# The first feed-forward's gate and up weights: every fourth float32r remainder summed by an accumulating DMA from SBUF

## The chip, the cores and the metric

The kernel runs on one core of one Trainium2 chip. The metric is the device time of one execution in microseconds (us), lower is better. The core's engines run side by side, each with its own instruction stream: TensorE (PE: matmuls; PEld: its weight loads), VectorE (DVE), ScalarE (ACT), GpSimd (POOL) and SyncE (SP, which here only issues loads). They wait for each other through semaphores. Sixteen DMA engines move the data for all of them.

## The reference, cut to what matters

One layer of a Conformer-like block over 256 tokens of width 2048: a first feed-forward, a mixing sublayer, cross-attention and a second feed-forward. The change touches the first half of the first feed-forward:

```python
h = rms_norm(x, ffn1_norm[l])
gate, up = jnp.split(h @ w_in, 2, axis=-1)          # w_in: 2048 x 11264
x = x + 0.5 * ((jax.nn.silu(gate) * up) @ w_out)    # w_out: 5632 x 2048
```

## The kernel before

All weights are float32 in HBM. TensorE multiplies float32r, a shorter float format, so every operand is split in two: `hi` is the value rounded to float32r, `lo` is the remainder `x - hi`, again rounded. Each product is then three matmuls: `hi` by `hi`, `hi` by `lo`, `lo` by `hi`.

The function `weights` makes such a pair for one weight tile of 128 x 1024 (512 KB): SP issues the load into a tile `raw` (four buffers), ACT copies it rounded into the first half of a tile `hl` (L104, three buffers), DVE subtracts that from `raw` into the second half (L105).

Gate and up of a feed-forward are computed by `swiglu_in` in 11 groups (`j`) of 512 gate and 512 up columns. A group takes 16 K tiles (`k`), each one load of 128 x 1024. For each K tile `by_two` issues 12 matmuls of 512 columns into four PSUM accumulators: four of line L258 (`hi` of the weights), four of L259 (`lo` of the weights), four of L262 (`lo` of the activations by `hi` of the weights). At the end of a group ACT applies SiLU to the gate (L274), DVE multiplies by up (L275), and PE transposes the result (L288) during the next group. The first group of the first feed-forward is written apart, in `first_group`: there the input `x` is loaded and split as well. Both feed-forwards call `swiglu_in`; `first` is not None in the first alone.

The order on each engine is set by the framework's scheduler when the kernel is built. Every instruction keeps its place in its engine's stream, so one that waits holds back all behind it.

Of the kernel before, what the change touches and what calls it, by code (L numbers as in the profile page):

```python
# [11 lines left out]
F32 = mybir.dt.float32  # L12
F32R = mybir.dt.float32r
AF = mybir.ActivationFunctionType
ALU = mybir.AluOpType
AX = mybir.AxisListType

P = 128
# [4 lines left out]
KD = D // P  # L23
# [38 lines left out]
def layer(ctx: ExitStack, tc: tile.TileContext, a: dict):  # L62
    nc = tc.nc
    out = a["out"]
# [19 lines left out]
    def beside(us):  # L84
        budget[0] = min(budget[0] + us, us) if later else 0.0
        while later and budget[0] > 0:
            cost, part = later.popleft()
            with tc.issue_after(newest[0].ins):
                part()
            budget[0] -= cost  # L90
# [6 lines left out]
    def weights(src, kk, n, hl=None):  # L97

        raw = wraw.tile([P, 1024], F32, name="raw")
        size = kk * n  # L100
        nc.sync.dma_start(out=raw[:, :size].rearrange("p (k n) -> p k n", n=n), in_=src)
        if hl is None:
            hl = whl.tile([P, 2, 1024], F32R, name="hl")
        nc.scalar.copy(out=hl[:, 0, :size], in_=raw[:, :size])  # L104
        newest[0] = nc.vector.tensor_tensor(  # L105
            out=hl[:, 1, :size], in0=raw[:, :size], in1=hl[:, 0, :size].bitcast(F32), op=ALU.subtract
        )
        v = hl[:, :, :size].rearrange("p two (k n) -> p two k n", n=n)
        return v[:, 0], v[:, 1]

    def split(hi, lo, x):
        nc.scalar.copy(out=hi, in_=x)
        nc.vector.tensor_tensor(out=lo, in0=x, in1=hi.bitcast(F32), op=ALU.subtract)
# [13 lines left out]
    def product_part(acc, w, k0, kk, x_hl, per, first, last, joint=False):  # L127

        hi, lo = weights(w[:, k0:k0 + kk, :], kk, P)
        for k in range(kk):  # L130
            f, l = first and k == 0, last and k == kk - 1
            (product_joint if joint else product)(acc, hi[:, k], lo[:, k], x_hl(k0 + k), f, l)
        beside(per)

    def gemm_t(w, x_hl, per=0.0, acc=None, ks=None, joint=False, between=None):

        return ahead([w], x_hl, per, [acc], ks, joint, between=between)[0]
# [14 lines left out]
    def gemm_n(w, x_hl, per=0.0, between=None):  # L152

        acc = [ps.tile([P, 2, 256], F32, name="acc").rearrange("p a b -> p (a b)") for _ in range(2)]
        nk = w.shape[1]
        for k0 in range(0, nk, 2):
            kk = min(2, nk - k0)
            hi, lo = weights(w[:, k0:k0 + kk, :], kk, 512)
            for k in range(kk):
                x = x_hl(k0 + k)  # L160
                for t in range(2):
                    s = slice(t * P, (t + 1) * P)
                    nc.tensor.matmul(acc[t], lhsT=x[:, 0, s], rhs=hi[:, k], start=k0 + k == 0, stop=False)  # L163
                    nc.tensor.matmul(acc[t], lhsT=x[:, 0, s], rhs=lo[:, k], start=False, stop=False)  # L164
                    nc.tensor.matmul(acc[t], lhsT=x[:, 1, s], rhs=hi[:, k], start=False, stop=k0 + k == nk - 1)  # L165
            if between and k0 >= 4:
                between.pop(0)()
            beside(per)
        return acc
# [65 lines left out]
    def gained_tile(norm):  # L235

        return big.tile([P, KD, 2, T], F32R, name="x_hl", tag="S")
# [11 lines left out]
    G = 512  # L249
    NG = F // G  # L250

    def by_two(acc, x, hi, lo, first, last):

        for t in range(2):
            s = slice(t * P, (t + 1) * P)
            for g in range(2):
                c = slice(g * G, (g + 1) * G)
                nc.tensor.matmul(acc[t][g], lhsT=x[:, 0, s], rhs=hi[:, c], start=first, stop=False)  # L258
                nc.tensor.matmul(acc[t][g], lhsT=x[:, 0, s], rhs=lo[:, c], start=False, stop=False)  # L259
            for g in range(2):  # L260
                c = slice(g * G, (g + 1) * G)
                nc.tensor.matmul(acc[t][g], lhsT=x[:, 1, s], rhs=hi[:, c], start=False, stop=last)  # L262

    def token_accs():
        return [[ps.tile([P, 2, 256], F32, name="acc").rearrange("p a b -> p (a b)") for _ in range(2)] for _ in range(2)]

    def swiglu_in(pool, x_hl, root, w_in, hA, hB, first, per):

        turns = []

        def gated(acc, r):
            h = pool.tile([P, 2, G], F32, name="h", bufs=2)
            for t in range(2):
                nc.scalar.activation(out=h[:, t], in_=acc[t][0], func=AF.Silu, scale=r[:, t:t + 1])  # L274
                nc.vector.scalar_tensor_tensor(  # L275
                    out=h[:, t], in0=acc[t][1], scalar=r[:, t:t + 1], in1=h[:, t], op0=ALU.mult, op1=ALU.mult
                )
            return h

        def turn(j, h, half):  # L280
            def go():
                f = 4 * j + 2 * half
                dst = hA[:, f:f + 2] if f < KD else hB[:, f - KD:f - KD + 2]
                tp = pa.tile([P, 2, T], F32, name="aux")
                for k in range(2):
                    for t in range(2):
                        c = slice((2 * half + k) * P, (2 * half + k + 1) * P)
                        nc.tensor.transpose(out=tp[:, k, t * P:(t + 1) * P], in_=h[:, t, c], identity=ident)  # L288
                split(dst[:, :, 0], dst[:, :, 1], tp)
            return go  # L290

        r = None
        for j in range(NG):
            if j == 0 and first is not None:
                acc = first()
            else:
                acc = token_accs()
                for k in range(KD):
                    hi, lo = weights(w_in[j, :, k:k + 1], 1, 2 * G)
                    by_two(acc, x_hl[:, k], hi[:, 0], lo[:, 0], k == 0, k == KD - 1)  # L300
                    if k in (3, 5) and turns:
                        turns.pop(0)()
                    beside(per)
            if r is None:
                r = root()
            h = gated(acc, r)
            turns += [turn(j, h, half) for half in range(2)]
        return turns

    def h_of(hA, hB):  # L310
        return lambda k: hA[:, k] if k < KD else hB[:, k - KD]


    x_hl = gained_tile("ffn1_norm")
# [31 lines left out]
    with tc.tile_pool(name="ffn1", bufs=1) as pool:  # L346
# [20 lines left out]
        x_hl = gained_tile("mix_norm")  # L367
        ss = st.tile([P, T], F32, name="ss", bufs=2)
        for f in range(KD):
            if f == 0:  # L370
                acc = gemm_t(a["ffn1_w_out"][f], h_of(hA, hB), between=turns)
            else:
                acc = gemm_t(a["ffn1_w_out"][f], h_of(hA, hB))
# [3 lines left out]
    with tc.tile_pool(name="mid", bufs=1) as mid:  # L377
        kT = mid.tile([P, KD, M], F32, name="kT")
        vv = mid.tile([P, 2, D], F32, name="vv")
        with tc.tile_pool(name="mix", bufs=1) as pool:  # L380
# [122 lines left out]
            for n in range(2):  # L503
                acc = gemm_n(a["w_mix_v"][n], lambda k: x_hl[:, k], per=1.35)
                for t in range(2):
                    nc.scalar.activation(
                        out=vs[:, t, n * 512:(n + 1) * 512], in_=acc[t], func=AF.Gelu, scale=r_t[:, t:t + 1]
# [57 lines left out]
            for f in range(KD):  # L565
                acc = gemm_t(a["w_k"][f], lambda k: m_hl[:, k], per=1.3, joint=True)
# [4 lines left out]
            for j in range(NCT):  # L571
                tu = ev.tile([P, T], F32, name="tu")
                acc = gemm_t(a["w_mix_in"][2 * NCT + j], lambda k: x_hl[:, k], per=0.9, joint=True)
# [23 lines left out]
            for h in range(HEADS):  # L597
                acc = gemm_n(a["w_v"][h], lambda k: m_hl[:, k], per=1.6)
                for t in range(2):
                    nc.scalar.activation(  # L600
                        out=vv[:, t, h * HD:(h + 1) * HD], in_=acc[t], func=AF.Copy, scale=r_mt[:, t:t + 1]
# [6 lines left out]
            x_hl = gained_tile("xattn_norm")  # L608
            ss = st.tile([P, T], F32, name="ss", bufs=2)
            for f in range(KD):  # L610
                if f < 3:
                    acc = gemm_t(a["w_mix_out"][f], lambda k: y_hl[:, k], acc=accs[f], ks=[(0, 8)])
                else:
                    acc = gemm_t(a["w_mix_out"][f], lambda k: y_hl[:, k])
# [3 lines left out]
        with tc.tile_pool(name="attn", bufs=1) as pool:  # L618
# [105 lines left out]
            x_hl = gained_tile("ffn2_norm")  # L724
            ss = st.tile([P, T], F32, name="ss", bufs=2)
            for f in range(KD):
                if f < 4:
                    acc = gemm_t(a["w_o"][f], o_of, acc=accs[f], ks=[(12, 4)] if f < 3 else [(8, 8)])
                else:
                    acc = gemm_t(a["w_o"][f], o_of)  # L730
# [3 lines left out]
    with ExitStack() as stack:  # L734
        pool = stack.enter_context(tc.tile_pool(name="ffn2", bufs=1))
# [15 lines left out]
        with tc.tile_pool(name="gate2", bufs=1) as gate:  # L751
            turns = swiglu_in(gate, x_hl, lambda: rms_cols(ss, D, "r_x2"), a["ffn2_w_in"], hA, hB, None, 0.4)
            finish()
            acc_0 = gemm_n(a["ffn2_w_out"][0], h, between=turns)
# [38 lines left out]
        for n in range(3):  # L793
            acc = gemm_n(a["ffn2_w_out"][n], h) if n else acc_0
# [6 lines left out]
        w = a["ffn2_w_out"][3]  # L801
        acc = [ps.tile([P, 2, 256], F32, name="acc").rearrange("p a b -> p (a b)") for _ in range(2)]
# [12 lines left out]
        for i, (k0, kk) in enumerate(parts):  # L815
            left = len(parts) - i
            hi, lo = weights(w[:, k0:k0 + kk, :], kk, 512, held[:, left - 1] if left <= 4 else None)
# [70 lines left out]
```

## Time and profile before

| | |
|---|---|
| median of 3 runs | 2161.44 us (2159.11 to 2161.5) |
| the profiled execution | 2160.25 us |
| its span in the trace | 2158.4 us |
| PE busy | 2137.0 us (99%) |
| DVE busy | 1311.4 us (61%) |
| ACT busy | 996.0 us (46%) |
| POOL busy | 13.3 us (1%) |
| DMA engines, share of the span | 62.5% by SP's queue |

The span is what the trace covers; the execution's own time is 1.85 us longer. A busy share is a mean over stages; whether an engine's work costs time is seen from who waits for it.

### The profile page before, as it was taken

The numbers are of one execution on the slowest core, as the hardware profiler recorded it, in microseconds if no ns is written. First come the engines' busy times: TensorE is split into PE (matmuls) and PEld (weight loads), VectorE is DVE, ScalarE is ACT, GpSimd is POOL, SyncE is SP. The second block draws the span as 40 slices with busy tenths as digits, with TensorE's granted clock in tenths as the row PEclk, the third lists the DMA queues.
The fourth block names the chain that finished last, engine by engine and source line by source line (L and its number), as shares of the span: only waits on it lengthen the run. The fifth ranks groups of instructions, "written<-read, shape, count | busy, mean of one in ns | idle before, by whom it ended". The sixth has DMA issues, their size and how long they took to land.

```text
span 2158.4 us, 28547 instructions
## 1 busy us (share of the span) xinstructions
PE 2137.0 (99%) x11164; PEld 1829.0 (85%) x11164; DVE 1311.4 (61%) x1705; ACT 996.0 (46%) x1232; POOL 13.3 (1%) x23
## 2 busy tenths in 40 slices
PE   8999999999999999999999999999999999999998
PEld 6788888888888899999888888888888888888886
DVE  5654454555555589888897666766644555444444
ACT  6544444444444453544575454544444444443443
POOL 0000000000000000000000000000000000000000
PEclk9999999999999999999999999999999999999999
DMA  8766666666666676565656653666666656666664
GB/s 276 225 188 192 189 192 183 192 190 181 187 188 188 199 234 193 183 177 185 187 184 195 185 157 118 196 193 186 188 193 187 193 181 193 192 206 192 188 191 149
DMA packets 114759, 409.95 MB, mean 190 GB/s; under 512 B 12864, under 2 KB 12992, under 8 KB 114496
## 3 DMA queue, kind: packets, MB, share of 16 engines
q1 hardware_dynamic: 114336, 407.35, 62.5%
q8 instruction: 87, 1.43, 0.3%
q10 hardware_dynamic: 288, 0.79, 0.1%
q14 instruction: 48, 0.39, 0.0%
HBM read 405.99 MB, written 2.10 MB: 189 GB/s over the span
## 4 chain that ended last, share of the span: by engine, by line
PE 95%; DMA 2%; DVE 1%; issue 1%; ACT 1%; SPq 0%; DVEq 0%; ACTq 0%
PE acc L117 16%; PE acc L258 14%; PE acc L262 14%; PE acc L259 14%; PE acc L118 8%; PE acc L165 5%; PE acc L163 5%; PE acc L164 5%; PE acc L125 3%; PE acc L124 3%; PE acc L123 3%; PE acc L811 1%; PE acc L813 1%; PE acc L812 1%; PE aux L288 1%; DMA raw<-in_x 1%
## 5 line engine op out<-in xcount | busy, mean ns | idle before, releaser
L105 DVE TENSOR_TENSOR hl<-raw,hl 128x1024 fp32r<-128x1024 f32 (+2 forms) x759 | 917.5, 1211 | 775.8 <-ACT hl L104 772.5
L104 ACT CAST hl<-raw 128x1024 fp32r<-128x1024 f32 (+2 forms) x759 | 785.5, 1038 | 1013.5 <-PE acc L262 504.7
L259 PE MATMUL acc<-hl,x_hl 128*128 128x512 f32 x1408 | 446.2, 391 | 0.5 <-DVE hl L105 0.5
L262 PE MATMUL acc<-hl,x_hl 128*128 128x512 f32 x1408 | 440.7, 390 | 0.0
L258 PE MATMUL acc<-hl,x_hl 128*128 128x512 f32 x1408 | 395.3, 393 | 9.7 <-ACT hl L104 8.0
L258 PEld LDWEIGHTS acc<-hl,x_hl 128*128 128x128 f32 x1408 | 261.6, 188 | 62.5 <-ACT hl L104 8.5
L262 PEld LDWEIGHTS acc<-hl,x_hl 128*128 128x128 f32 x1408 | 264.5, 188 | 55.4
L259 PEld LDWEIGHTS acc<-hl,x_hl 128*128 128x128 f32 x1408 | 262.8, 188 | 55.1 <-DVE hl L105 1.4
L117 PE MATMUL acc<-hB,hl 128*128 128x512 f32 x448 | 158.9, 397 | 0.0
L118 PE MATMUL acc<-hB,hl 128*128 128x256 f32 x448 | 125.9, 281 | 0.0
L123 PE MATMUL acc<-x_hl,hl 128*128 128x256 f32 x384 | 108.7, 283 | 0.5 <-ACT hl L104 0.5
L125 PE MATMUL acc<-x_hl,hl 128*128 128x256 f32 x384 | 108.2, 283 | 0.9 <-DVE hl L105 0.7
L124 PE MATMUL acc<-x_hl,hl 128*128 128x256 f32 x384 | 108.5, 283 | 0.0
L117 PEld LDWEIGHTS acc<-hB,hl 128*128 128x128 f32 x448 | 84.1, 188 | 20.4
L117 PE MATMUL acc<-x_hl,hl 128*128 128x512 f32 x256 | 90.6, 396 | 0.0
L117 PE MATMUL acc<-o_hl,hl 128*128 128x512 f32 x256 | 90.2, 398 | 0.0
L117 PE MATMUL acc<-hA,hl 128*128 128x512 f32 x256 | 89.8, 392 | 0.0
L117 PE MATMUL acc<-y_hl,hl 128*128 128x512 f32 x256 | 89.0, 394 | 0.0
L118 PEld LDWEIGHTS acc<-hB,hl 128*128 128x128 f32 x448 | 84.5, 189 | 0.0
L125 PEld LDWEIGHTS acc<-x_hl,hl 128*128 128x128 f32 x384 | 73.4, 192 | 1.3 <-DVE hl L105 1.3
L123 PEld LDWEIGHTS acc<-x_hl,hl 128*128 128x128 f32 x384 | 73.7, 192 | 0.8 <-ACT hl L104 0.7
L124 PEld LDWEIGHTS acc<-x_hl,hl 128*128 128x128 f32 x384 | 73.7, 192 | 0.0
(229 smaller groups left out, 2830.1 us busy)
## 6 DMA issues: line engine op xcount, KB each, us to landing
raw<-in_ffn_w_in SPq DMA_DIRECT2D x352, 512.0 KB, 3.6
raw<-in_ffn_w_out SPq DMA_DIRECT2D x120, 512.0 KB, 3.8
raw<-in_ffn_w_out SPq DMA_DIRECT2D x64, 448.0 KB, 3.5
raw<-in_w_mix_in SPq DMA_DIRECT2D x48, 512.0 KB, 4.6
raw<-in_w_k SPq DMA_DIRECT2D x32, 512.0 KB, 3.8
raw<-in_w_v SPq DMA_DIRECT2D x32, 512.0 KB, 3.7
raw<-in_w_mix_out SPq DMA_DIRECT2D x32, 512.0 KB, 4.5
raw<-in_w_q SPq DMA_DIRECT2D x32, 512.0 KB, 4.5
```

Source lines behind the costliest of these rows:

```text
L104: nc.scalar.copy(out=hl[:, 0, :size], in_=raw[:, :size])
L105: newest[0] = nc.vector.tensor_tensor(out=hl[:, 1, :size], in0=raw[:, :size], in1=hl[:, 0, :size].bitcast(F32), op=ALU.subtract)
L117: nc.tensor.matmul(acc, lhsT=w_hi, rhs=x_hl, start=first, stop=False, skip_group_check=True)
L118: nc.tensor.matmul(acc[:, 0], lhsT=w_lo, rhs=x_hl[:, 0], start=False, stop=last, skip_group_check=True)
L123: nc.tensor.matmul(d, lhsT=w_hi, rhs=x_hl[:, 0], start=first, stop=False, skip_group_check=True)
L124: nc.tensor.matmul(d, lhsT=w_hi, rhs=x_hl[:, 1], start=False, stop=False, skip_group_check=True)
L125: nc.tensor.matmul(d, lhsT=w_lo, rhs=x_hl[:, 0], start=False, stop=last, skip_group_check=True)
L163: nc.tensor.matmul(acc[t], lhsT=x[:, 0, s], rhs=hi[:, k], start=k0 + k == 0, stop=False)
L164: nc.tensor.matmul(acc[t], lhsT=x[:, 0, s], rhs=lo[:, k], start=False, stop=False)
L258: nc.tensor.matmul(acc[t][g], lhsT=x[:, 0, s], rhs=hi[:, c], start=first, stop=False)
L259: nc.tensor.matmul(acc[t][g], lhsT=x[:, 0, s], rhs=lo[:, c], start=False, stop=False)
L262: nc.tensor.matmul(acc[t][g], lhsT=x[:, 1, s], rhs=hi[:, c], start=False, stop=last)
```

## The change

In groups 1 to 10 of the first feed-forward, the K tiles 3, 7, 11 and 15 (40 tiles in all) no longer go through `weights` but through a new function, `weights_summed`. It loads the tile into `raw_s` (two buffers), ACT writes its negative, rounded, into the second half of a tile `hl_s` (one buffer) and then the rounded value into the first half. GpSimd then issues a DMA from `raw_s` to that second half which adds to what stands there: `-hi + raw`. So the remainder comes from a DMA within SBUF, and DVE has nothing to do for that tile. The call stands at `k % 4 == 0`, three K tiles ahead of the use. The first group, the second feed-forward and every other product stay as they are.

```diff
+    def weights_summed(pool, src, n):
+
+        raw = pool.tile([P, n], F32, name="raw_s", bufs=2)
+        nc.sync.dma_start(out=raw, in_=src)
+        hl = pool.tile([P, 2, n], F32R, name="hl_s", bufs=1)
+        nc.scalar.activation(out=hl[:, 1], in_=raw, func=AF.Copy, scale=-1.0)
+        nc.scalar.copy(out=hl[:, 0], in_=raw)
+        nc.gpsimd.dma_start(out=hl[:, 1], in_=raw, accum_op=ALU.add)
+        return hl[:, 0], hl[:, 1]
...
                 for k in range(KD):
-                    hi, lo = weights(w_in[j, :, k:k + 1], 1, 2 * G)
-                    by_two(acc, x_hl[:, k], hi[:, 0], lo[:, 0], k == 0, k == KD - 1)
+                    if first is not None and k % 4 == 0:
+                        summed = weights_summed(pool, w_in[j, :, k + 3], 2 * G)
+                    if first is not None and k % 4 == 3:
+                        hi, lo = summed
+                    else:
+                        hi, lo = [w[:, 0] for w in weights(w_in[j, :, k:k + 1], 1, 2 * G)]
+                    by_two(acc, x_hl[:, k], hi, lo, k == 0, k == KD - 1)
```

In the changed kernel lines 111 and on have moved: L116 is the negation, L117 the rounded copy, L118 the accumulating DMA, L114 the load of `raw_s`, and the matmuls of L258, L259 and L262 are L268, L269 and L272. In the rows below a semaphore named DMAHW counts loads issued by SP, DMASW the DMAs issued by GpSimd, and Activation, DVE and PE the instructions of these engines.

ScalarE's stream in the second group, before: one rounded copy for each K tile, each waiting for its load and for PE to leave an `hl` buffer.

```order
L104 CAST hl<-raw 128x1024 [waits DMAHW0_49,DVE_49,PE_49]
L104 CAST hl<-raw 128x1024 [waits DMAHW1_49,DVE_49,PE_49]
L104 CAST hl<-raw 128x1024 [waits DMAHW2_49,DVE_49,PE_49]
L104 CAST hl<-raw 128x1024 [waits DMAHW3_49,DVE_49,PE_49]
L274 ACTIVATE h<-acc,r_x_92 128x512 [waits PE_49] x2
```

The same stretch in the changed kernel, from the negation for K tile 11 of that group to the copy for K tile 15:

```order
L116 ACTIVATE hl_s<-raw_s 128x1024 [waits DMASW1_49,PE_49,Activation_49]
L117 CAST hl_s<-raw_s 128x1024
L104 CAST hl<-raw 128x1024 [waits DMAHW6_49,DVE_49,PE_49]
L104 CAST hl<-raw 128x1024 [waits DMAHW7_49,DVE_49,PE_49]
L104 CAST hl<-raw 128x1024 [waits DMAHW1_49,DVE_49,PE_49]
L116 ACTIVATE hl_s<-raw_s 128x1024 [waits DMASW2_49,DMAHW0_49,PE_49,Activation_49]
L117 CAST hl_s<-raw_s 128x1024
```

Every fourth copy has become a negation and a copy; the negation waits for PE to have left the one `hl_s` buffer, that is for the last matmul of the summed tile before, and the copies for the three tiles of the other kind (8, 9 and 10 ahead of tile 11) stand ahead of it.

TensorE's stream for one K tile, before: it waits for ACT's copy, and after four matmuls for DVE's remainder.

```order
L258 MATMUL acc<-hl,x_hl 128x512 [waits Activation_49]
L258 MATMUL acc<-hl,x_hl 128x512 x3
L259 MATMUL acc<-hl,x_hl 128x512 [waits DVE_49]
L259 MATMUL acc<-hl,x_hl 128x512
L262 MATMUL acc<-hl,x_hl 128x512 x2
L259 MATMUL acc<-hl,x_hl 128x512 x2
L262 MATMUL acc<-hl,x_hl 128x512 x2
```

In the changed kernel, K tile 11 of the second group, a summed one, and the beginning of K tile 12, which is not:

```order
L268 MATMUL acc<-hl_s,x_hl 128x512 [waits Activation_49]
L268 MATMUL acc<-hl_s,x_hl 128x512 x3
L269 MATMUL acc<-hl_s,x_hl 128x512 [waits DMASW2_49]
L269 MATMUL acc<-hl_s,x_hl 128x512
L272 MATMUL acc<-hl_s,x_hl 128x512 x2
L269 MATMUL acc<-hl_s,x_hl 128x512 x2
L272 MATMUL acc<-hl_s,x_hl 128x512 x2
L268 MATMUL acc<-hl,x_hl 128x512 [waits Activation_49]
L269 MATMUL acc<-hl,x_hl 128x512 [waits DVE_49]
```

The count of matmuls is the same; the fifth of a summed tile now waits for the accumulating DMA, and in the other tiles L268 and L269 often alternate.

SyncE's stream in the first group, before (`xT` and `in_x` are the input):

```order
L101 DMA raw<-in_ffn_w_in 128x1024
L332 DMA xT<-in_xT 128x512
L101 DMA raw<-in_ffn_w_in 128x1024 x4
L322 DMA raw<-in_x 128x1024
L101 DMA raw<-in_ffn_w_in 128x1024 x2
```

and in the changed kernel:

```order
L101 DMA raw<-in_ffn_w_in 128x1024
L347 DMA xT<-in_xT 128x512
L114 DMA raw_s<-in_ffn_w_in 128x1024
L101 DMA raw<-in_ffn_w_in 128x1024
L114 DMA raw_s<-in_ffn_w_in 128x1024
L101 DMA raw<-in_ffn_w_in 128x1024 x3
L337 DMA raw<-in_x 128x1024
L101 DMA raw<-in_ffn_w_in 128x1024 x2
L114 DMA raw_s<-in_ffn_w_in 128x1024
```

Three loads for the second group's K tiles 3, 7 and 11 have moved up into the first group; the third needs the buffer of the first, so SP holds it until the first accumulating DMA has landed.

## Rows read from the trace of the kernel before

**Rows 1.** The profile's page: busy time, share of the span and instructions of each engine, and the chain of work that ended last, by engine.
```profile
PE 2137.0 (99%) x11164; PEld 1829.0 (85%) x11164; DVE 1311.4 (61%) x1705; ACT 996.0 (46%) x1232; POOL 13.3 (1%) x23
...
PE 95%; DMA 2%; DVE 1%; issue 1%; ACT 1%; SPq 0%; DVEq 0%; ACTq 0%
```

**Rows 2.** Stretches of the first feed-forward's gate and up: the stretch in us, its length, then busy time (instructions) of PE, PEld, DVE, ACT and POOL, the granted TensorE clock as a share of full speed, the DMA engines' share and GB/s. The first two hold the first group and the start of the second, the third is about one group, the last the groups from the third on.
```profile
0.00:54.00 54.00, 45.96 (x194) 37.16 (x194) 27.39 (x41) 32.51 (x49) 0.70 (x6) 1.00 0.80 275
54.00:100.00 46.00, 43.84 (x196) 35.72 (x196) 28.74 (x37) 25.03 (x36) 0.00 (x0) 1.00 0.73 232
100.00:143.00 43.00, 43.00 (x195) 35.55 (x194) 21.65 (x20) 18.03 (x20) 0.00 (x0) 1.00 0.65 192
...
100.00:444.00 344.00, 344.00 (x1549) 284.32 (x1548) 172.25 (x156) 147.20 (x156) 0.00 (x0) 1.00 0.64 189
```

**Rows 3.** What PE waited for from 0 to 490 us: waiter, releaser, us in total, times, longest.
```profile
PE acc L258 <- ACT hl L104: 8.0, 2, 7.3
PE acc L258 <- ACT h L274: 1.6, 1, 1.6
PE acc L259 <- DVE hl L105: 0.5, 1, 0.5
```

**Rows 4.** The costly groups from 100 to 444 us on DVE and ACT: count, busy us, mean ns of one, idle time before them and who ended it.
```profile
L105 DVE TENSOR_TENSOR hl<-raw,hl 128x1024 fp32r<-128x1024 f32 x124 | 151.2, 1225 | 171.0 <-ACT hl L104 171.0
...
L104 ACT CAST hl<-raw 128x1024 fp32r<-128x1024 f32 x124 | 129.7, 1053 | 191.3 <-PE acc L262 191.3
```

**Rows 5.** PE in order of time (start us, duration of the merged piece in us): four transposes and the tile behind them, the start of a later tile, one whole tile with the next tile's start, and a stretch of single matmuls in mixed order.
```profile
109.53 0.60 PE L288 MATMUL aux<-ident,h 128*128 128x128 f32 x4
109.89 1.18 PE L258 MATMUL acc<-hl,x_hl 128*128 128x512 f32 x4
...
115.45 0.84 PE L258 MATMUL acc<-hl,x_hl 128*128 128x512 f32 x3
...
129.05 1.07 PE L258 MATMUL acc<-hl,x_hl 128*128 128x512 f32 x4
129.95 0.62 PE L259 MATMUL acc<-hl,x_hl 128*128 128x512 f32 x2
...
131.77 1.07 PE L258 MATMUL acc<-hl,x_hl 128*128 128x512 f32 x4
...
147.41 0.39 PE L259 MATMUL acc<-hl,x_hl 128*128 128x512 f32 x1
147.63 0.39 PE L262 MATMUL acc<-hl,x_hl 128*128 128x512 f32 x1
147.86 0.39 PE L258 MATMUL acc<-hl,x_hl 128*128 128x512 f32 x1
```

**Rows 6.** ACT in order of time: an ACTIVATE over 128 x 1024 (the squares of `x`), the two SiLU pieces at a group's end, and a copy in the middle of a group; in brackets the idle time before and who ended it.
```profile
26.07 1.06 ACT L323 ACTIVATE raw<-raw 128x1024 f32<-128x1024 f32 x1 [2.42 <-DMA raw<-in_x]
...
99.94 0.69 ACT L274 ACTIVATE h<-acc,r_x 128x512 f32<-128x512 f32 x1 [0.53 <-PE acc L262]
100.85 0.69 ACT L274 ACTIVATE h<-acc,r_x 128x512 f32<-128x512 f32 x1 [0.22 <-PE acc L262]
...
115.65 1.05 ACT L104 CAST hl<-raw 128x1024 fp32r<-128x1024 f32 x1 [1.67 <-PE acc L262]
```

**Rows 7.** Loads: the queue of SP over the whole span (packets, MB, share of 16 engines); then issues by destination and source with count, KB each and median us from issue to landing: 100 to 444 us, 5 to 25 us (where the next group shows the DMA engines full), and one pair of 512 KB loads of the whole span; last, minimum, median and maximum of the loads of 100 to 444 us.
```profile
q1 hardware_dynamic: 114336, 407.35, 62.5%
...
raw<-in_ffn_w_in SPq DMA_DIRECT2D x122, 512.0 KB, 3.7
...
raw<-in_ffn_w_in SPq DMA_DIRECT2D x7, 512.0 KB, 5.4
...
gb<-in_sgu_ln SPq DMA_DIRECT2D x2, 512.0 KB, 10.1
...
DMA to landing us min/median/max: 3.4/3.7/5.1
```

**Rows 8.** The first group: a stretch of five us (columns as in rows 2), SP's second issue of `in_x` in order of time, the copies of K tiles 8 and 9 on ACT, their remainders on DVE, and PE at K tile 8.
```profile
10.00:15.00 5.00, 5.00 (x23) 4.09 (x22) 4.03 (x7) 4.08 (x8) 0.00 (x0) 1.00 1.05 397
...
27.25 0.33 SPq L322 DMA_DIRECT2D raw<-in_x  x1
...
27.13 1.99 ACT L104 CAST hl<-raw 128x1024 fp32r<-128x1024 f32 x2
28.19 2.36 DVE L105 TENSOR_TENSOR hl<-raw,hl 128x1024 fp32r<-128x1024 f32 x2 [3.29 <-ACT hl L104]
30.55 1.07 PE L258 MATMUL acc<-hl,x_hl 128*128 128x512 f32 x4
31.46 0.62 PE L259 MATMUL acc<-hl,x_hl 128*128 128x512 f32 x2
```

## The prediction

> **What bounds the kernel now.** I read the page's head first: PE is busy 99% of the span, and the chain of work that ended last runs 95% through PE, 1% through DVE [rows 1]. Then the stage that the change touches, by stretches: in every stretch from 100 us on PE is busy for its whole length at full clock, 344.00 of 344.00 us, while DVE works half of the time (172.25) and ACT 147.20 [rows 2]. What PE waits for in the whole first feed-forward's gate and up comes to 10.1 us, 7.3 of them the very first wait, before anything has been loaded; 0.5 us are put down to DVE [rows 3]. DVE itself sits idle 171.0 us in these 344, for ACT's copies, and ACT 191.3 us, for PE to give back a buffer [rows 4]. So the order of dependence is PE, then ACT, then DVE: DVE is late for nobody. One K tile takes PE 2.72 us (129.05 to 131.77), a matmul 0.23 us, in whatever order the lines follow one another (147.41, 147.63, 147.86) [rows 5].
>
> **What is removed.** 40 remainders of 1.225 us on DVE [rows 4], 49 us of busy time. On the path they are worth nothing: PE's own instructions cover them, and PE keeps the same 12 matmuls for each tile. If that cover were gone (DVE behind PE), it would show as waits on DVE, and those are 0.5 us in all [rows 3]. The waits of the second group's beginning, 8.0 + 1.6 + 0.5 less the first 7.3, are 2.8 us; that is all the stage could give back.
>
> **What is added at no cost.** ACT gets 40 negations, about 1.06 us each by the nearest row, an ACTIVATE over 128 x 1024 [rows 6]: 42 us in a stage where ACT stands still for more than half of the time. The copies of the three ordinary tiles stand ahead of a negation in ACT's stream and wait only for older buffers, so the negation holds back none that PE needs before the summed tile. The mixed order of matmuls costs nothing (0.23 us each in either order, above). The number of loads is the same; a quarter of them moves to the two buffers of `raw_s`. SP may stand up to one accumulate long at such a load, with the loads of the next tiles behind it; with four `raw` and three `hl` buffers these run several tiles of 2.72 us ahead, and 3.7 us to landing [rows 7] leaves room.
>
> **What is added on the path: the wait for the accumulating DMA.** There is one `hl_s`, so the negation for the next summed tile can begin only when PE has finished the last one, and PE needs the sum three tiles later. The time between is a budget that I work out from rows:
>
> - ACT starts 0.20 us after PE begins the next tile (a copy at 115.65 released by PE, PE's next tile at 115.45) [rows 5, 6]. The negation takes 1.06, so the DMA can be issued at 1.26.
> - PE needs the sum at three tiles and four matmuls: 3 x 2.72 + 0.91 (129.05 to 129.95) = 9.07 us [rows 5].
> - Budget from issue to landing: 9.07 - 1.26 = 7.8 us for K tiles 11 and 15. For K tile 7 PE's order reads the sum after one matmul (0.68 earlier), but seven transposes of 0.09 us (four in 109.53 to 109.89) stand between: 7.8 too. These are 30 tiles.
> - K tile 3: at a group's end one SiLU of 0.69 us, released by the same last matmul, stands ahead of the negation on ACT (100.85) [rows 6]; with one transpose in between the budget is 9.07 + 0.09 - 1.95 = 7.2 us. These are 9 tiles (the second group's is made far ahead).
>
> Every us beyond the budget is a us of PE's, and nothing gives it back, since PE is the bound before and behind.
>
> How long the accumulate takes no row of before shows: GpSimd issues no DMA there. From below: no load of 512 KB in this stage lands in less than 3.4 us, 3.7 in the median [rows 7]. A load reads 512 KB and writes 512 KB; an accumulate reads two and writes one, so half as much again: 5.6 us when nothing else is in the way, inside both budgets. From above: the same loads land in 5.4 us where the engines are full, 5 to 25 us [rows 7]; twice that, if the two reads go one after the other, is 10.8, and the slowest 512 KB load of the kernel takes 10.1 [rows 7]. In between: 5.4 x 1.5 = 8.1 us. I take 8.1, because the accumulate does not run alone: loads hold the engines for 0.64 of the stage [rows 2], and the accumulate brings more (one load is 0.625 x 2158.4 us x 0.524 / 407.35 MB = 1.74 us of all 16 engines [rows 7]; half as much again in every four tiles of 10.9 us is 0.24, so 0.88 in all), which is nearer to the full engines than to the lone load. The Trainium skill says the same in DMA: Bandwidth & Descriptors, section Issuing engines are not separate DMA queues: DMAs of SP, ACT and GpSimd run on the same 16 engines and interleave, so another issuer saves only issuing time. By a row the sharing shows as 5.4 against 3.7 us on one queue; no row here shows it between two.
>
> **The sum.** At 8.1 us: 9 x (8.1 - 7.2) + 30 x (8.1 - 7.8) = 8 + 9 = 17 us. The profiled execution took 2160.25 us, 1.85 more than its span, and lies 1.2 below the median 2161.44 of the runs. 2160.25 + 17 = 2177 us. The bounds: at 5.6 us nothing; at 10.8, 9 x 3.6 + 30 x 3.0 = 122 us.
>
> **The start.** Three loads for the second group move into the first group, where the engines are full (1.05 at 397 GB/s from 10 to 15 us) [rows 8]: at that rate 1.32 us each, 4 us for the loads behind them. SP holds the third until the first accumulate has landed; ACT works off that negation around 20 us, so the accumulate ends near 28, about where SP issues its second load of `x` (27.25). The remainder of K tile 8 is ready at about 29.4 and PE reads it at 31.46 [rows 8]: 2.1 us of slack. So the cost is between nothing (and a gain of at most the 2.8 us above, if the second group's start closes up) and some 2 to 4 us. I take nothing, as three loads fewer follow when the second group begins, and keep 4 for the range.
>
> **The rivals.**
> - *The accumulate lands in time* (not slower). The place is the same wait; it decides at 7.2 us from issue to landing. For it: the lone load's 3.7 us, with one further read of 1.74 us of all engines, makes 5.4 [rows 7], and the lone 1.5-fold 5.6. Against it: engines that are 0.64 taken [rows 2]. Then nothing moves: 2160 us. Two rules of the Trainium skill speak for this case: DMA: Bandwidth & Descriptors, section Anatomy of one DMA, puts a GpSimd-issued DMA at about 2.0 us + bytes / 436 GB/s; Collectives: The Full Stack, section The bandwidth ceiling, says that the add costs only its second read (62.28 against 32.35 GB/s). An estimate by these pages is 2.0 + 2 x 1.2 = 4.4 us; no run here shows it.
> - *The accumulate is much slower than a load* (over 10.8 us). Its adds, or GpSimd's making of descriptors, would set the pace. No row speaks for or against it. At 13 us: 9 x 5.8 + 30 x 5.2 = 208 us, 2368 us.
> - *The start alone costs*, at the moved loads and SP's hold: 2160 + 4 = 2164 us, and over 0.2% only if SP's hold adds to it.
> - *The start closes up* and the accumulates fit: 2160 - 2.8 = 2157 us, still within 0.2%. That the change would win by taking work off DVE has no row: DVE's waits are 0.5 us.
>
> **How the numbers follow.** 0.2% (4.3 us) is about what a measurement of this kernel can tell from no change. Accumulate late, 7.5 to 10.8 us: 0.48, the likeliest, 2177 us, own range 2163 to 2270. In time, start neutral: 0.38. Much slower: 0.06. Start costs: 0.05. Start closes up: 0.03. Of the late case about 0.03 stays below 4.3 us. Slower: 0.45 + 0.06 + 0.03 = 0.54; faster 0.03; the same 0.43. The range for 8 in 10 goes from 2158 (the median less a little, for the in-time case) up to 2270 (10.4 us: 9 x 3.2 + 30 x 2.6 = 107 us), leaving out the much slower case, the last of the late one and the gain.
>
> **What would show it.** In the profile of the changed kernel: PE's L269 on `hl_s` waiting for a DMA, some 40 times, about 0.9 us at K tile 3 and 0.3 at the others; from issue to landing about 8 us for `hl_s<-raw_s`; the DMA share from 0.64 to about 0.88 in 100 to 444 us; DVE's busy time 49 us lower and ACT's 42 higher; PE's other waits as before. Wrong it would be if the landing is under 7.2 us (no such waits, 2160), if SP's hold makes ordinary tiles late (PE waiting for ACT's copies), or if the negation starts later than 0.2 us behind PE.

## The result and the profile after

| | before | changed |
|---|---|---|
| median | 2158.51 us (2157.58 to 2162.23, 20 runs) | 2163.61 us (2160.16 to 2166.38, 20 runs) |
| ratio, 95% interval | | 1.002 (1.0014 to 1.0026) |
| profiled execution, its span | 2160.25 us, 2158.4 us | 2161.57 us, 2159.8 us |

The medians lie 5 us apart (0.24%), and the ratio says 0.20%: clear of no change, but less than a third of the 17 us forecast. The head, the queues and the chain of the changed kernel's page:

```profile
PE 2139.1 (99%) x11164; PEld 1829.5 (85%) x11164; DVE 1263.8 (59%) x1665; ACT 1030.9 (48%) x1270; POOL 48.1 (2%) x63
...
q1 hardware_dynamic: 114336, 407.35, 60.6%
q0 software_dynamic: 5760, 20.97, 5.0%
...
PE 96%; DMA 0%; DVE 0%; ACT 0%; issue 0%; DVEq 0%
```

DVE is 47.6 us less busy and ACT 34.9 more than in [rows 1]; the chain runs through PE as before. (The 20 runs put the kernel before 3 us lower than the three runs ahead of the prediction.) The stage, 100 to 444 us, in the columns of [rows 2]:

```profile
100.00:444.00 344.00, 344.00 (x1536) 282.11 (x1536) 134.28 (x124) 174.80 (x186) 26.88 (x31) 1.00 0.79 236
```

Its DMA issues in the columns of [rows 7], the loads first:

```profile
raw<-in_ffn_w_in SPq DMA_DIRECT2D x91, 512.0 KB, 4.8
hl_s<-raw_s POOLq DMA_DIRECT2D x31, 512.0 KB, 5.0
```

The landing times of `hl_s`, minimum, median and maximum over the kernel:

```profile
DMA to landing us min/median/max: 4.5/5.0/9.7
```

PE never waits here, and the accumulate lands in 5.0 us in the median, not 8.1. What PE waited for from 0 to 490 us (columns of [rows 3]):

```profile
PE acc L268 <- ACT hl L104: 7.1, 1, 7.1
PE acc L269 <- DMA hl_s<-raw_s: 2.8, 1, 2.8
PE acc L268 <- ACT h L284: 0.7, 1, 0.7
```

There is one wait for the DMA, not 39. It belongs to the second group's K tile 7. In order of time, SP's issues, GpSimd's and PE's (start us, duration):

```profile
58.63 13.31 SPq L101 DMA_DIRECT2D raw<-in_ffn_w_in  x8
...
68.27 0.87 POOL L118 DMA_DIRECT2D hl_s<-raw_s  x1 [47.21 <-ACT hl_s L116]
...
78.00 0.73 PE L269 MATMUL acc<-hl_s,x_hl 128*128 128x512 f32 x2 [2.84 <-DMA hl_s<-raw_s]
```

SP issues eight loads from 58.63 us to 71.94; the accumulate is issued in the midst of them and lands 9.7 us later. The next summed tile, K tile 11, already runs without a wait, as all later ones do (ACT, GpSimd, PE):

```profile
80.22 1.06 ACT L116 ACTIVATE hl_s<-raw_s 128x1024 fp32r<-128x1024 f32 x1 [4.91 <-PE acc L272]
...
81.57 0.86 POOL L118 DMA_DIRECT2D hl_s<-raw_s  x1 [12.43 <-ACT hl_s L116]
...
85.41 0.39 PE L268 MATMUL acc<-hl,x_hl 128*128 128x512 f32 x1
...
88.13 1.10 PE L268 MATMUL acc<-hl_s,x_hl 128*128 128x512 f32 x4
89.07 0.63 PE L269 MATMUL acc<-hl_s,x_hl 128*128 128x512 f32 x2
...
90.93 0.39 PE L268 MATMUL acc<-hl,x_hl 128*128 128x512 f32 x1
```

From issue to need are 81.57 to 89.07, 7.50 us (predicted 7.8). But the tile itself took 88.13 to 90.93, 2.80 us, where the tile ahead of it took 2.72 (85.41 to 88.13), as a tile of before does [rows 5].

Comparing the start of the same matmul in the two traces splits the stage, which ends 4.3 us later: 0.6 lost at the very first tiles, where a load of `raw_s` now stands ahead of K tile 1's (that this is the cause is not shown); 3.0 gained up to 60 us, where the second group's start closes up; 3.2 lost at the late tile; then 0.36 lost in each group, 0.09 for each summed tile, 3.5 us in all.

Behind the stage the two traces come together again: 1.8 us between 750 and 889 us, where the kernel before has two waits (0.5 and 0.7 us) that the changed kernel has not, and 1.3 us between 1314 and 1416 us. So the two spans end only 1.4 us apart. The profiled execution of before lies 1.7 us above its median and that of the changed kernel 2.0 below; how much of this comes back in a median execution is not known. The split is that of one pair of traces.

The 3.0 us at the second group's start can be placed in ACT's stream. Before, the copy for the group's first K tile (52.39) stands behind the squares of `memT`, whose load ACT waits for; the third row is DVE's remainder for K tile 3:

```profile
51.45 0.42 ACT L203 ACTIVATE sm<-raw 128x256 f32<-128x256 f32 x1 [2.38 <-DMA raw<-in_memT]
...
52.39 1.98 ACT L104 CAST hl<-raw 128x1024 fp32r<-128x1024 f32 x2
...
63.70 1.23 DVE L105 TENSOR_TENSOR hl<-raw,hl 128x1024 fp32r<-128x1024 f32 x1 [0.36 <-ACT hl L104]
```

In the changed kernel that copy stands ahead of them:

```profile
49.00 1.03 ACT L104 CAST hl<-raw 128x1024 fp32r<-128x1024 f32 x1
50.06 0.42 ACT L213 ACTIVATE sm<-raw 128x256 f32<-128x256 f32 x1
```

The remainder of 63.70 us is the first that the change takes off DVE, and by then the gain has been made. So it does not come from relieving DVE but goes with the loads moved into the first group, which changed the order of the streams. In every traced kernel of the layer that makes tiles by `weights_summed` the copy stands ahead, in every other one behind.

### The profile page after: what moved, and what is told of

The parts are those of the page before. It is cut to its first block, busy times and chain, and to the rows that moved or that the text cites. A ratio compares the mean times of both kernels' runs of the same rounds, so it can differ in the third digit from the quotient of the medians.

```text
span 2159.8 us, 28628 instructions
## 1 busy us (share of the span) xinstructions
PE 2139.1 (99%) x11164; PEld 1829.5 (85%) x11164; DVE 1263.8 (59%) x1665; ACT 1030.9 (48%) x1270; POOL 48.1 (2%) x63
## 4 chain that ended last, share of the span: by engine, by line
PE 96%; DMA 0%; DVE 0%; ACT 0%; issue 0%; DVEq 0%
PE acc L127 16%; PE acc L269 14%; PE acc L272 14%; PE acc L268 14%; PE acc L128 8%; PE acc L175 5%; PE acc L173 5%; PE acc L174 5%; PE acc L135 4%; PE acc L134 4%; PE acc L133 4%; PE acc L826 1%; PE acc L828 1%; PE acc L827 1%; PE aux L298 1%; DMA hl_s<-raw_s 0%
## 5 line engine op out<-in xcount | busy, mean ns | idle before, releaser
L105 DVE TENSOR_TENSOR hl<-raw,hl 128x1024 fp32r<-128x1024 f32 (+2 forms) x719 | 868.9, 1211 | 796.4 <-ACT hl L104 791.5
L104 ACT CAST hl<-raw 128x1024 fp32r<-128x1024 f32 (+2 forms) x719 | 742.7, 1036 | 931.5 <-PE acc L272 422.4
L269 PE MATMUL acc<-hl,x_hl 128*128 128x512 f32 x1248 | 426.9, 391 | 0.0
L268 PE MATMUL acc<-hl,x_hl 128*128 128x512 f32 x1248 | 396.7, 393 | 7.8 <-ACT hl L104 7.1
L272 PE MATMUL acc<-hl,x_hl 128*128 128x512 f32 x1248 | 390.5, 390 | 0.0
L268 PEld LDWEIGHTS acc<-hl,x_hl 128*128 128x128 f32 x1248 | 232.4, 188 | 54.9 <-ACT hl L104 7.1
L272 PEld LDWEIGHTS acc<-hl,x_hl 128*128 128x128 f32 x1248 | 234.8, 188 | 49.5
L269 PEld LDWEIGHTS acc<-hl,x_hl 128*128 128x128 f32 x1248 | 234.0, 188 | 48.5
```

Source lines behind the costliest of these rows:

```text
L105: newest[0] = nc.vector.tensor_tensor(out=hl[:, 1, :size], in0=raw[:, :size], in1=hl[:, 0, :size].bitcast(F32), op=ALU.subtract)
```

## The experiments

Two theories of the slow tiles stood at first. **Height**: the second stage of the same trace shows `hB`, whose address is high in SBUF as that of `hl_s` is, at 233 ns a matmul and `hA`, which lies low, at 227. **DMA**: what a DMA has written, or traffic beside the matmul, slows it. The medians of before that share a chip with each run are given, since they differ a little between chips.

**hl_s at a low address.** The pools `wraw`, `ev` and `st` go to the far end, and `hl_s` gets the room ahead of `hB`.

```diff
-    wraw = ctx.enter_context(tc.tile_pool(name="wraw", bufs=4))
+    wraw = ctx.enter_context(tc.tile_pool(name="wraw", bufs=4, side="right"))
...
-        hl = pool.tile([P, 2, n], F32R, name="hl_s", bufs=1)
+        hl = nears[0].tile([P, 2, n], F32R, name="hl_s", bufs=1)
```

> The changed kernel with hl_s at a low SBUF address (110144 to 118336 bytes of a partition in place of 218656), by moving wraw, ev and st to the far end; hB moves down with it (134720 in the first feed-forward, 110144 in the second). Theory of the address: a matmul that reads an operand far up in SBUF starts its successor after 233 ns instead of 227; hl_s tiles then take 2.72 us as the others do, the gate/up stage loses 3.2 to 3.5 us, and hB's ten lowest K tiles give some 1.6 us more in the last stage: about 2158.6. Theory of the DMA (the matmuls are slow because their operand was written by the accumulating DMA, or because its traffic runs beside them): hl_s tiles stay at 2.80 us, about 2162.

2158.14 us beside a before of 2159.33; ratio 0.9995 (0.9986 to 1.0004). The summed tiles run at 227.4 ns a matmul, mean of 465. So it is not the DMA. But `hB` in the last stage, from 110144 to 167488, was at 226.7 ns throughout, although its upper two fifths lie where before it was slow (144928 to 202272): height is in doubt too.

**DVE's sums in a high tile.** The kernel before, with every fourth pair in a tile `hl_s` high in SBUF. As there is no `raw_s`, it lies 8 KB lower than in the changed kernel, at 210464.

```diff
-                    hi, lo = weights(w_in[j, :, k:k + 1], 1, 2 * G)
+                    far = None
+                    if first is not None and k % 4 == 3:
+                        far = pool.tile([P, 2, 2 * G], F32R, name="hl_s", bufs=1)
+                    hi, lo = weights(w_in[j, :, k:k + 1], 1, 2 * G, far)
```

> The kernel before with every fourth K tile's hi/lo pair of groups 1 to 10 in a tile named hl_s at the changed kernel's address, filled by ScalarE and VectorE as ever; no second DMA. Theory of the address: 40 tiles at 2.80 instead of 2.72 us, 480 matmuls times 6.6 ns = 3.2 us, about 2161.7. Theory of the DMA: 2158.5, hl_s tiles at 2.72 us.

2162.92 us beside 2159.33; 1.0015 (1.0006 to 1.0024), 3.6 us. The tiles run at 233.5 ns without any DMA. The place of the tile is the cause, whoever fills it.

**Without the one late tile.**

```diff
-                    if first is not None and k % 4 == 0:
+                    if first is not None and k % 4 == 0 and (j, k) != (1, 4):
...
-                    if first is not None and k % 4 == 3:
+                    if first is not None and k % 4 == 3 and (j, k) != (1, 7):
```

> The changed kernel with the one tile whose landing was late (second group, K tile 7) left to VectorE. If the 2.8 us wait belongs to the burst of eight loads at the second group's start alone, it goes: about 2160.7. If it only moves to the next summed tile (K tile 11), about 2163.6.

2159.41 us beside 2159.33; 0.9998 (0.9989 to 1.0006). PE's waits from 0 to 490 us:

```profile
PE acc L268 <- ACT hl L104: 7.2, 1, 7.2
PE acc L268 <- ACT h L284: 1.0, 1, 1.0
```

The wait is gone and went to no other tile. The sum issued in the burst of loads is now K tile 11's (at 68.25 us); it still takes 9.7 us to land, but PE needs it 17 us after its issue.

**Without the accumulating DMA.** The one line that issues it is left out; the second half of `hl_s` then holds only the negated rounding.

```diff
-        nc.gpsimd.dma_start(out=hl[:, 1], in_=raw, accum_op=ALU.add)
```

> The changed kernel without the accumulating DMA (the second part then holds only the negated rounding, so the output lacks the correction of those tiles). All that is left is ScalarE's negation, the address and the order. Theory of the address: hl_s tiles still 2.80 us, the 2.8 us wait gone: about 2160.7. Theory of the DMA: hl_s tiles at 2.72 us: about 2157.4.

2160.64 us beside 2159.33; 1.0009 (1.0000 to 1.0018). The summed tiles are still at 233.5 ns. With DVE's 40 remainders gone and no DMA in their place, the kernel is no faster than before. In its trace the second group's start gives back 2.3 us and the offset takes about 3.5 in the groups behind, as in the changed kernel; the removed 49 us of DVE show no gain beside these.

**Every second tile.** Only the spacing is changed (`k % 2` for `k % 4`, `k + 1` for `k + 3`).

> The changed kernel with every second K tile of groups 1 to 10 summed by the DMA (80 tiles). The one hl_s buffer is then free two tiles later in the cycle, so the time from issue to the first need falls from 7.4 us to 7.4 - 2 x 2.72 = 2.0 us. With the price that the trace of the changed kernel shows, 5.0 us: 3.0 us of wait a tile, 80 times, some 240 us, about 2400. With the price taken in the prediction, 8.1 us: 6.1 us a tile, about 2650. If the landing were hidden whatever the budget: about 2165.

2427.09 us (two runs) beside 2158.94; 1.1242 (1.1221 to 1.1262). What PE waited for in the stage, from 100 to 740 us:

```profile
PE acc L269 <- DMA hl_s<-raw_s: 148.2, 70, 4.2
```

The same stretch in the columns of [rows 2]:

```profile
100.00:740.00 640.00, 488.40 (x1775) 368.05 (x1774) 114.19 (x117) 237.23 (x252) 61.65 (x71) 0.89 0.66 174
```

One summed tile in order of time, GpSimd and PE:

```profile
202.34 0.86 POOL L118 DMA_DIRECT2D hl_s<-raw_s  x1 [9.23 <-ACT hl_s L116]
...
207.11 1.19 PE L269 MATMUL acc<-hl_s,x_hl 128*128 128x512 f32 x2 [2.98 <-DMA hl_s<-raw_s]
208.09 1.05 PE L272 MATMUL acc<-hl_s,x_hl 128*128 128x512 f32 x2
208.94 1.05 PE L269 MATMUL acc<-hl_s,x_hl 128*128 128x512 f32 x2
...
210.63 0.39 PE L268 MATMUL acc<-hl,x_hl 128*128 128x512 f32 x1
```

Now the budget is too short and nearly every summed tile waits, 2.1 us in the mean: here the budget is 1.8 us (202.34 to 207.11 less 2.98) and the landing 4.8. The predicted mechanism is real, with the short price. The total fits the expected 2400 partly by chance. The waits are 148 of the 268 us added, shorter than the 3.0 us a tile expected, and a second cost joins them: behind many of the waits some matmuls take 0.43 us each (208.09 to 208.94 for two), half the rate. The granted clock is 0.50 from 208.0 to 210.6 us, the lower level of 1.2 GHz, and 0.89 over the stage. Behind the one wait of 2.84 us in the changed kernel it stayed at 1.00.

**hB low in the kernel before.** `xT`, `pv`, `wraw`, `ev` and `st` to the far end, no DMA sums.

> The kernel before with xT, pv, wraw, ev and st moved to the far end of SBUF, so that hB starts at 92288 bytes of a partition instead of 144928. Nothing else is changed. Theory of the address, with a bound somewhere between 126528 and 144928: 17 to 25 of hB's 28 K tiles of the second feed-forward's last step come down from 233 to 227 ns a matmul, 24 matmuls each: 2.7 to 4.0 us, and as much or less in the first one's: about 2155.5. If the address is not the cause: 2158.5.

2157.94 us beside 2158.94; 0.9995 (0.9986 to 1.0004), undecided as a time. In the trace every matmul on `hB` of the last stage runs at 226.7 ns, also those on its last 5 KB (to 149632), which lay high enough for 233 before. (The first down projection took 1.6 us longer; see the padding below.)

**A map of addresses.** Runs of 16 matmuls, the moving operand at 72 to 200 KB, then the stationary one; the start of each run in us is the first column.

> Not the layer: runs of 16 matmuls of 512 float32r columns whose moving operand (then whose stationary operand) lies at rising addresses, after 60 matmuls at low ones; the tiles' names give the address in KB. Theory of the address: 227 ns a matmul up to a bound between 124 and 142 KB and 233 ns above, for the moving operand and for the stationary one. If only certain tiles are slow, no bound is seen.

```profile
21.42 3.79 PE L76 MATMUL acc<-at96k,at8k 128*128 128x512 f32 x16
25.05 3.79 PE L76 MATMUL acc<-at104k,at8k 128*128 128x512 f32 x16
...
75.82 3.79 PE L76 MATMUL acc<-at200k,at8k 128*128 128x512 f32 x16
79.45 3.79 PE L76 MATMUL acc<-at40k,at72k 128*128 128x512 f32 x16
```

Each run takes 3.63 us, 227 ns a matmul, at 96 KB as at 200. Height falls as a cause. All of these tiles start at a multiple of 64 bytes, and so do `hA`, `x_hl` and `hl`. `hl_s` at 218656 (in `dve_high` at 210464) and `hB` at 144928 start 32 bytes past one; in the two kernels with shifted pools (`low` and the last one) the starts are multiples of 64. That is the third theory, **offset**.

**The offset alone, both kernels.** One small tile becomes 64 bytes wide, which shifts all pools behind it by 32 bytes; in the changed kernel also with `hl_s` alone shifted.

```diff
-    nc.scalar.activation(out=st.tile([P, 1], F32, name="warm"), in_=ones[:, 0:1], func=AF.Silu)
+    nc.scalar.activation(out=st.tile([P, 16], F32, name="warm")[:, 0:1], in_=ones[:, 0:1], func=AF.Silu)
```

> The kernel before with the one-element tile warm made 64 bytes wide, which moves every later tile of the pool st and of all pools behind it by 32 bytes and nothing else: hB starts at 144960 (a multiple of 64) in place of 144928 (32 past one). Theory of alignment (a matmul with an operand that starts 32 bytes past a multiple of 64 costs 6.6 ns more, wherever it lies): the last step's 671 matmuls on hB come down from 233.3 to 226.7 ns, 4.4 us, and the first down projection's by 1 to 2 us: 2153 to 2155 beside a kernel before of 2159. If height and not alignment were the cause: no change.

> The changed kernel with the same 32 bytes of padding: hl_s at 218688 in place of 218656, hB at 144960. Theory of alignment: hl_s tiles at 2.72 us though they lie as high as before and are written by the DMA, 3.2 us in the gate/up stage, and what pad gains behind it: 2155 to 2157 beside a kernel before of 2159. If height or the DMA were the cause: hl_s tiles stay at 2.80 us.

> The changed kernel with hl_s alone moved by 32 bytes (a wider tile, its first eight elements unused); all else stays where it was. Theory of alignment: 480 matmuls times 6.6 ns = 3.2 us less than the changed kernel, about 2160.5 beside a kernel before of 2159, with hB still at 233.3 ns. Otherwise no change.

Beside a before of 2158.23 us: `pad` 2154.54, 0.9984 (0.9975 to 0.9993); `after_pad` 2155.96, 0.9991 (0.9982 to 1.0000); `after_hls` 2159.05, 1.0004 (0.9996 to 1.0013). Shifting `hl_s` by 32 bytes takes its tiles to 227.0 ns and leaves `hB` at 233.3. A summed tile there, and the next tile's start:

```profile
87.12 1.07 PE L268 MATMUL acc<-hl_s,x_hl 128*128 128x512 f32 x4
...
89.84 0.39 PE L268 MATMUL acc<-hl,x_hl 128*128 128x512 f32 x1
```

2.72 us (87.12 to 89.84) in place of 2.80. Twelve matmuls on `hB` in the last stage, in the kernel before and then in `pad` (the row after the gap begins the thirteenth):

```profile
1939.74 0.40 PE L165 MATMUL acc<-hl,hB 128*128 128x512 f32 x1
...
1942.54 0.40 PE L165 MATMUL acc<-hl,hB 128*128 128x512 f32 x1
```

```profile
1940.21 0.39 PE L164 MATMUL acc<-hl,hB 128*128 128x512 f32 x1
...
1942.93 0.39 PE L164 MATMUL acc<-hl,hB 128*128 128x512 f32 x1
```

2.80 against 2.72 us; over 671 matmuls of the last stage that is the 4.4 us expected. The 1 to 2 us expected of the first down projection did not come; `pad` lost 1.6 us there, and so did every other kernel in which `hB` starts at a multiple of 64. Its 512- and 256-column matmuls on `hA` alternate in pairs of 348 ns before and 353 with the padding, though the start of `hA` had not moved; the pairs on `hB` took 353 and 354. Why is open. `after_hls` is the cleanest test for the changed kernel, since nothing but `hl_s` moves.

**Offsets apart.** Runs of 24 matmuls; the names give the bytes past a multiple of 64 of the moving and the stationary operand.

> Not the layer: runs of 24 matmuls, all operands at low addresses; the moving operand, then the stationary one, starts 4, 8, 16, 32, 48 and 60 bytes past a multiple of 64 (the tiles' names give it). Theory of alignment: 226.7 ns at 0 and 233.3 ns at 32 bytes for either operand; what the other offsets and both at once cost is open. Otherwise 226.7 ns throughout.

```profile
39.59 5.76 PE L77 MATMUL acc<-mov32b,sta0b 128*128 128x512 f32 x24
45.19 5.75 PE L77 MATMUL acc<-mov48b,sta0b 128*128 128x512 f32 x24
50.78 5.61 PE L77 MATMUL acc<-mov60b,sta0b 128*128 128x512 f32 x24
56.22 5.75 PE L77 MATMUL acc<-mov0b,sta4b 128*128 128x512 f32 x24
...
72.94 5.76 PE L77 MATMUL acc<-mov0b,sta32b 128*128 128x512 f32 x24
78.54 5.76 PE L77 MATMUL acc<-mov0b,sta48b 128*128 128x512 f32 x24
...
89.74 5.63 PE L77 MATMUL acc<-mov32b,sta32b 128*128 128x512 f32 x24
95.20 5.61 PE L77 MATMUL acc<-mov32b,sta16b 128*128 128x512 f32 x24
100.65 8.50 PE L77 MATMUL acc<-mov0b,sta0b 128*128 128x512 f32 x48
```

From start to start, divided by 24: the moving operand alone at 32 bytes 233 ns (39.59 to 45.19), the stationary one alone 233 (72.94 to 78.54). Both at 32 give 227.5 (89.74 to 95.20): an offset of 32 is not slow as such, it depends on the other operand's start. What the rule is, the runs do not tell: a moving operand at 32 with a stationary one at 16, and 60 with 0, are fast too (227), while 0 with 60 is slow (233). At 256 columns the runs show no such cost (117 to 120 ns).

**The price of the accumulate.** 512 KB each, alone, then issued behind loads.

> Not the layer: transfers of 512 KB each, every phase alone behind a barrier: one accumulating DMA from SBUF to SBUF on the POOL queue, one plain copy on it, one plain copy and one load on SP's queue, and an accumulating DMA issued right behind one, four and eight loads. If the price of the accumulation is the memory path itself, it takes about 5 us alone and no more than 5.5 beside one load; behind eight loads it takes the 9.7 us of the one late tile. If reading the destination costs a second pass (the 1.5 of the prediction), the accumulating one takes half as long again as the plain copy.

One round, in the columns of [rows 7]; the three `acc` rows stand behind one, four and eight loads:

```profile
acc_alone<-src POOLq DMA_DIRECT2D x1, 512.0 KB, 4.7
plain_pool<-src POOLq DMA_DIRECT2D x1, 512.0 KB, 2.9
plain_sp<-src SPq DMA_DIRECT2D x1, 512.0 KB, 2.9
load_alone<-in_ffn_w_in SPq DMA_DIRECT2D x1, 512.0 KB, 3.7
...
acc<-src POOLq DMA_DIRECT2D x1, 512.0 KB, 5.7
...
acc<-src POOLq DMA_DIRECT2D x1, 512.0 KB, 10.0
...
acc<-src POOLq DMA_DIRECT2D x1, 512.0 KB, 10.2
```

Against the plain copy the accumulate takes 1.6 times as long (4.7 by 2.9), but the base is a copy within SBUF, 2.9 us, and not a load. One load ahead of it costs 1.1 to 1.6 us (5.7 to 6.1 in three rounds, more than the 5.5 allowed for). Four loads make it 10.0 us, about twice the time and close to the late tile's 9.7; eight cost no more than four.

**Both costs out.** `skip_pad` is the changed kernel without the late tile and with the 32 bytes of padding; `one_group` keeps the DMA sum only in the second group (`j == 1`).

> The changed kernel with both costs taken out: K tile 7 of the second group left to VectorE (skip_one) and the 32 bytes of padding (pad). Beside a kernel before of 2159: pad alone gave 2154.5 of 2158.2; the second group's start closes up by 2 to 3 us, nothing is left to pay: about 2152. If the removed VectorE work costs as much elsewhere as the start gives: 2154.5.

> skip_pad with the DMA sum in the second group alone (its K tiles 3, 11 and 15); the 36 tiles of the later groups go back to VectorE. If VectorE's work is worth nothing where PE never waits and only the second group's start gains: the same as skip_pad within 1 us, about 2152. If the later tiles earn something too: slower than skip_pad, 2154 or more.

Beside a before of 2159.41 us: `skip_pad` 2152.51, 0.9968 (0.9956 to 0.9981); `one_group` 2153.27, 0.9971 (0.9961 to 0.9982). Both are faster than the kernel before. Both also lie below `pad`'s 0.9984, but the intervals overlap, so a gain beyond the padding is not shown by the times. The 36 tiles of the later groups are worth nothing that can be told. In the traces PE is 2.6 us (`skip_pad`) and 3.1 us (`one_group`) ahead of the kernel before at the second group's K tile 6, and 0.8 in `pad`: what gain there is beyond the padding belongs to the second group's start.

## Why the prediction was wrong

**What bounds the kernel**: right. PE is busy 344.00 of 344.00 us in the stage after as before, and without any sum in place of DVE's (`no_sum`) nothing is won beyond the second group's start.

**What is added at no cost**: right as far as it went. ACT's negation takes 1.06 us and starts 0.25 us after PE begins the next tile (predicted 0.20); the mixed order costs nothing (2.72 us a tile); the loads land later (4.8 against 3.7 us) and make no ordinary tile late.

**The budgets**: right in method, up to 0.4 us too long. Measured from issue to need: 7.1 us for K tile 3, 7.5 for K tile 7, 7.4 in the median for the others (predicted 7.2 and 7.8). GpSimd's issue follows the end of the negation by 0.3 to 0.4 us, which the sum left out. `every_second` shows the mechanism with a budget of 1.8 us.

**The failed step**: "I take 8.1." The factor of 1.5 was good (1.6 measured), the base was not: 5.4 us is a load from HBM behind a full queue, and an SBUF copy takes 2.9. The argument for the upper end, that a stage with the engines at 0.88 is like the first microseconds, where they are full, failed too: the share came to 0.79, and the accumulate took 5.0 in the median, hardly more than its 4.5 to 4.7 alone. Of the prices worked out from rows the lowest, 5.4 and 5.6 us, were the nearest, and they still lay above what came. So 39 waits of 0.3 to 0.9 us became one of 2.8, and the rival that lands in time (2160) had the mechanism right for 38 of the 39 tiles; the nearest of these landed 0.6 us ahead of PE's need (6.5 of 7.1 us). The estimate of 4.4 us by the Trainium skill (DMA: Bandwidth & Descriptors, section Anatomy of one DMA, and Collectives: The Full Stack, section The bandwidth ceiling) agrees with the 4.5 to 4.7 us alone in the total; of its parts the copy, estimated at 3.2 us, measured 2.9, and the second read, estimated at 1.2 us, measured 1.6 to 1.8. The Trainium skill's rule that issuers share the engines (DMA: Bandwidth & Descriptors, section Issuing engines are not separate DMA queues) agrees with the 10.0 us behind four loads of SP's.

**The missed terms.** The late tile: it is a wait of the forecast kind, but at one tile. The prediction counted on three loads fewer as the second group begins; eight were issued there in 13 us. In every traced kernel with every fourth tile summed, the sum issued among them landed in 9.4 to 10.2 us, and PE waited only where that was K tile 7's (not in `skip_one`). `dma_price` has the same 10 us behind four loads; no run moved the burst itself. The offset: "the same 12 matmuls" put a summed tile's own time at 2.72 us, but its matmuls ran at 233 instead of 227 ns: 480 x 6.6 ns = 3.2 us by the sizes, 3.5 by the traces, and `after_hls` takes it away. The prediction followed instructions and transfers, not where the new tile was put; the rows of before had the clue only in a stage that the change does not touch.

**The start**: taken as 0 within -2.8 and +4. It gave back 3.0 us, about the 2.8 us of waits that were named as the most that the stage could give [rows 3]; of these waits 2.1 us went and one of 0.7 stayed, and the other 0.9 us is not accounted for. So in the traces the stage's cost is -3.0 + 0.6 + 3.2 + 3.5 = 4.3 us, near the 5 of the medians. The small number is a sum of terms of both signs, and the term that the forecast was made of, the wait at every summed tile, is not among them. That it lies between the two likeliest cases, 2160 and 2177, is luck.

## What to carry to other kernels

Price a new transfer from the same path (SBUF to SBUF here), and price it twice, in the steady stage and in the busiest burst that it can fall into; a budget that holds 38 times may fail once, and that once costs all that it lacks. When an operand gets a new tile, look up where the tile starts and compare the time of one tile with its neighbours' before reading any wait: with 32 bytes `after_hls` took the ratio to the kernel before from 1.0020 to 1.0004. Work taken off an engine that nobody waits for gained nothing that these runs can tell; the one gain, at the second group's start, came before that engine was relieved, so look at what else a change moves in the streams.

## What the runs showed of the hardware

- Two float32r operands that start at different offsets within 64 bytes can cost 6.6 ns a matmul of 512 columns (233.3 against 226.7 ns); 0 with 32 bytes cost it in either order, 32 with 32 and 32 with 16 did not, and height in SBUF (72 to 200 KB) did not matter. The full rule is open. The kernel before paid it on `hB` for 671 matmuls; 32 bytes of padding made it 0.16% faster (0.9975 to 0.9993).
- An accumulating DMA of 512 KB within SBUF lands in 4.5 to 4.7 us alone, 5.7 to 6.1 behind one load, and 10.0 to 10.2 behind four or eight; a plain copy takes 2.9 from GpSimd's queue and from SP's. GpSimd is busy 0.87 us in issuing the one and 0.56 in issuing the other (medians of `dma_price`).
- In `every_second`, with waits of 2.1 us in the mean and up to 4.2, the matmuls behind many of the waits ran at the lower clock level, 1.2 GHz (0.43 us each), and the granted clock of the stage was 0.89; behind the one wait of 2.8 us in the changed kernel it stayed at 1.00.
